# Down products of four feed-forward blocks: three groups of rows instead of two, placed in another order

## The chip, the cores and the metric

One core of one Trainium2 chip runs the kernel. The metric is the device time of one launch in microseconds (us); less is better. TensorE does the matrix products, VectorE (DVE) and ScalarE (ACT) the elementwise work, GpSimd (POOL) one small power function, and SyncE (SP) issues the transfers.

## What is computed

Two layers of an encoder on 512 positions of width 1024, in float32. Each layer is a feed-forward block, a mixing block and a second feed-forward block, each with an RMS norm ahead of it and a residual add behind it; a last RMS norm follows. The change concerns the four feed-forward blocks (width 2816):

```
def swiglu(h, w_gate, w_up, w_down):
    return (jax.nn.silu(h @ w_gate) * (h @ w_up)) @ w_down
...
    for l in range(DEPTH):
        x = x + 0.5 * swiglu(rmsnorm(x, g_ffn1[l]), w_ffn1_gate[l], w_ffn1_up[l], w_ffn1_down[l])
        ...                      # mixing block: Fourier, dilated and differential attention, gates
        x = x + 0.5 * swiglu(rmsnorm(x, g_ffn2[l]), w_ffn2_gate[l], w_ffn2_up[l], w_ffn2_down[l])
    return rmsnorm(x, g_final)
```

## The kernel before, in words

Activations lie with features on the 128 partitions and the 512 positions along the free axis. Each float32 operand is held as a high and a low part; a product is three matmuls (`mm3`, L186: low by high, high by low, high by high), all into one PSUM accumulator.

**Feed-forward block** (`ffn`, L533). The width 2816 is 22 blocks of 128, called rows here. For each row `tile_ops` (L541) pushes a gate product and an up product: 8 blocks of the input by 3 matmuls of 512 columns each, so 48 matmuls for a row. Behind the up product, `act` (L552) multiplies by the norm's row factors, applies silu and multiplies gate by up.

**Down products.** `FGROUPS` (L35) splits the 22 rows into (0, 12) and (12, 22). Behind the gate and up products of a group come its down products, in one of two forms.

- The form of seven products (`quad_ops`, L601): two output blocks and two rows at a time, with the positions in two halves of 256, done as 7 products in place of 8. `seven` (L340) builds sums and differences of two rows, with high and low parts, in 3.5 tiles of the `pairs` pool (21 buffers); `load` (L207) adds up the weights on DVE and splits 7 blocks into parts; the products go into 4 accumulators, and `combine` (L626) puts them together on DVE and adds to `x`. Output blocks come in 4 sets (o = 0, 2, 4, 6); a set is loaded in pieces of up to 4 rows.
- The plain form (`down_ops`, L575): one output block at a time, 3 matmuls per row. In the last block of the network it is done for each half of the positions by itself (256 columns), so that the final norm (`LastNorm`, L499) can begin on one half.

Before, all rows of the first three feed-forward blocks take the form of seven products; in the last block rows 0 to 11 do, and rows 12 to 21 are plain in halves.

**Order.** Work that needs weights is an `Op` in a queue (`push`, L258). `fill` (L277) takes one, emits the weight work of the next one too, then whatever waits in `later` (the `combine` of a finished set), then the products. Other work, such as the statistics of a norm, are generators (`spawn`, L263), each with a due time; `step` (L295) advances one when its due time is at or below `est.time`, the running sum of what matmuls are taken to cost. Due times come from `Estimate` and `_Engine` (L94 to L126), which add up costs of ACT and DVE instructions in the order in which they are emitted, each from the result of the one before (`est.ready`). `Norm.ready` (L475) drives a generator to its end at once, whatever its due time. At the end of a block `drain` (L306) empties the queue before the next block pushes its own.

**Norm.** When output block k of `x` is final, `Norm.block` (L471) makes its high and low parts (ACT, DVE) and adds its square to a sum (ACT, DVE). Behind the eighth block `square` (L450) spawns `stats` (L462): four small matmuls with ones, DVE, the power function on POOL, ACT, DVE (`diagonals`, L414), then two matmuls (`bcast`, L427) that spread the factors.

Of the kernel before, what the change touches and what calls it, by code (L numbers as in the profile page):

```python
# [14 lines left out]
ALU = mybir.AluOpType  # L15
# [19 lines left out]
FGROUPS = ((0, 12), (12, 22))  # L35
# [94 lines left out]
def encoder_kernel(ctx: ExitStack, tc: tile.TileContext, I: dict, out: bass.AP):  # L130
# [50 lines left out]

    def mm(ps, w, xx, start, stop, us):
        T.matmul(ps, w, xx, start=start, stop=stop)  # L183
        est.pe(us)

    def mm3(ps, w, xx, start, stop, us=0.216):  # L186

        mm(ps, w[1], xx[0], start, False, us)
        mm(ps, w[0], xx[1], False, False, us)
        mm(ps, w[0], xx[0], False, stop, us)  # L190

    class Op:
# [14 lines left out]
        def load(self, cuts=1):  # L207
# [3 lines left out]
            if self.sums:  # L211
# [6 lines left out]
                self.w = []  # L218
                for r in raws:
                    V.tensor_tensor(r[:, 4:6], r[:, 1:4:2], r[:, 0:1].to_broadcast([P, 2, P]), op=ALU.add)  # L220
                    V.tensor_tensor(r[:, 6], r[:, 4], r[:, 3], op=ALU.add)
                    V.tensor_tensor(r[:, 7], r[:, 6], r[:, 2], op=ALU.add)
                    w = [t.rearrange("p (s c) -> p s c", s=7) for t in self.parts(896)]
                    split(*w, r[:, 1:])
                    self.w.append(w)
# [8 lines left out]
            self.w = []  # L234
            for a in range(0, n, per):
                e = min(n, a + per)
                hi, lo = self.parts(e - a)
                self.w.append((hi, lo))
                some = max(1, cuts // 2)
                for c in range(some):  # L240
                    cs = slice((e - a) * c // some, (e - a) * (c + 1) // some)
                    split(hi[:, cs], lo[:, cs], raw[:, a:e][:, cs])
                    if cuts > 1:
                        yield
# [95 lines left out]
    def seven(te, to, share):  # L340
# [10 lines left out]
        A.activation(a[:, 0], te[:, 0], AF.Copy)  # L351
        V.tensor_tensor(s0[:, 0], te[:, 1], te[:, 0], op=ALU.subtract)
        V.tensor_tensor(s0[:, 1], te[:, 1], to[:, 1], op=ALU.subtract)
        A.activation(a[:, 1:3], to, AF.Copy)
        V.tensor_tensor(s1[:, 0], te[:, 0], s0[:, 1], op=ALU.subtract)
        V.tensor_tensor(s1[:, 1], to[:, 0], s1[:, 0], op=ALU.subtract)
        A.activation(sh[:, 0:2], s0, AF.Copy)
        V.tensor_tensor(a[:, 3], te[:, 0], f(a[:, 0]), op=ALU.subtract)
        A.activation(sh[:, 2:4], s1, AF.Copy)
# [74 lines left out]
    class Norm:  # L434
# [8 lines left out]
        def pairs(self, k):  # L443
            p = xpair()
            A.activation(p[:, 0], x[:, k, :], AF.Copy, scale=gain(self.i, k))
# [4 lines left out]
        def square(self, k):  # L450
            if self.n == 0:
                self.sum = npool.tile([P, 512], F32, tag="sum", name=nm("sum"))
                A.activation(self.sum, x[:, k, :], AF.Square)
            else:
                sq = tmp()
                A.activation(sq, x[:, k, :], AF.Square)
                V.tensor_add(self.sum, self.sum, sq)
            self.n += 1
            if self.n == KD:
                self.chain = spawn(self.stats(), est.ready)  # L460
# [72 lines left out]
    def ffn(l, which, norm, nxt):  # L533
# [3 lines left out]
        last = isinstance(nxt, LastNorm)  # L537
        forms = [not (last and j >= FGROUPS[1][0]) for j in range(NF)]
        share = []

        def tile_ops(j):  # L541
# [6 lines left out]
            def up(w):  # L548
# [3 lines left out]
                def act():  # L552
# [11 lines left out]
                    else:  # L564
                        hs[j] = b
                        e = j - j % 2
                        if hs[e] is not None and hs[e + 1] is not None:
# [7 lines left out]
        def down_ops(o, f0, f1, half=None):  # L575
            mid = (f0 + f1 + 1) // 2
            po = []
            cs = slice(0, 512) if half is None else slice(half * 256, half * 256 + 256)
            us = 0.216 if half is None else 0.108
# [18 lines left out]
            part(f0, mid)  # L598
            part(mid, f1)

        def quad_ops(o, f0, f1):  # L601
            po = []

            def part(a0, a1):
                def body(w):
# [3 lines left out]
                    if a1 == f1:  # L609
                        def done():  # L610
                            combine(po, o)
                            if f1 == NF:
                                nxt.block(o)
                                nxt.block(o + 1)

                        if f1 == NF and o == KD - 2:
                            done()
                        else:
                            later.append(done)
# [22 lines left out]

        for f0, f1 in FGROUPS:
            for j in range(f0, f1):
                tile_ops(j)
            if forms[f0]:
                for o in range(0, KD, 2):
                    quad_ops(o, f0, f1)
            else:
                for half in (0, 1):  # L650
                    for o in range(KD):
                        down_ops(o, f0, f1, half)
# [35 lines left out]
    def token_major(l, norm, name, n, evict):  # L688
# [3 lines left out]
        def body(kk):  # L692
            def go(w):
                if kk == 0:
                    ps.extend(acc() for _ in range(NTB))
                for tb in range(NTB):
                    for k2 in range(2):
# [3 lines left out]
                        mm3(ps[tb][:, :n], xx, ww, k == 0, k == KD - 1, 0.216 * n / 512)  # L701
# [575 lines left out]
```

## Time and profile before

| | |
|---|---|
| Median of 3 runs | 2508.38 us (2500.59, 2508.38, 2508.8) |
| Profiled execution, its own time | 2503.38 us |
| Span of its trace | 2501.5 us |
| Granted clock of TensorE, mean | 0.986 of full |
| TensorE matmul busy | 2440.1 us (98%), 12902 instructions |
| VectorE busy | 1653.8 us (66%) |
| ScalarE busy | 1079.3 us (43%) |
| Chain that ended last | 90% TensorE, 7% VectorE |

The busy time of an engine is the time in which it executed instructions; matmuls are pipelined, so their busy time overlaps and hides gaps shorter than one matmul. A granted clock below 1 in a stretch means that TensorE ran there at half of its full clock for a part of it: its two levels are 2.4 and 1.2 GHz.

### The profile page before, as it was taken

Reading aid. Unit: us, or ns where it says so; the run is one execution under the profiler, and the core shown is the slowest. Engines: PE = TensorE matmul, PEld = TensorE weight load, DVE = VectorE, ACT = ScalarE, POOL = GpSimd, SP = SyncE. Lnnn points to the kernel's source line nnn. Section 1 sums busy time; section 2 is a strip of 40 time slices with the busy share of each in tenths; the row PEclk is TensorE's granted clock in tenths of the full one; section 3 lists DMA queues with packets and bytes.
Section 4 is the critical chain, followed back from the end, with each engine's and each line's share of the span. In section 5 each row is a group of like instructions: output and inputs, shape, how many; then the busy total and the mean of one; then the engine's idle time right before and its main releaser. Section 6 shows DMA issues by size and latency. Waiting matters only on the chain.

```text
span 2501.5 us, 33775 instructions
## 1 busy us (share of the span) xinstructions
PE 2440.1 (98%) x12902; PEld 2099.5 (84%) x12902; DVE 1653.8 (66%) x3254; ACT 1079.3 (43%) x1858; POOL 20.6 (1%) x24
## 2 busy tenths in 40 slices
PE   8999999999999999999999999999999999999997
PEld 6788898878887888988978988888888878889887
DVE  5687694545776656866956867845467656568556
ACT  4343353544544434433533434445455444334344
POOL 0000000000000000000000000000000000000000
PEclk9999999999999999999999999999999999999998
DMA  4333233212321323332322332331222213324334
GB/s 147 130 108 122 81 108 111 80 61 83 103 76 59 97 93 101 84 120 81 108 91 89 97 118 84 107 115 60 74 94 87 90 44 113 99 80 118 101 94 142
DMA packets 88850, 240.85 MB, mean 96 GB/s; under 512 B 10009, under 2 KB 17945, under 8 KB 88688
## 3 DMA queue, kind: packets, MB, share of 16 engines
q1 hardware_dynamic: 88688, 238.69, 30.3%
q8 instruction: 101, 1.65, 0.3%
q14 instruction: 61, 0.50, 0.1%
HBM read 235.41 MB, written 6.91 MB: 97 GB/s over the span
## 4 chain that ended last, share of the span: by engine, by line
PE 90%; DVE 7%; ACT 1%; DMA 1%; issue 1%; POOL 0%; SPq 0%; POOLq 0%; ACTq 0%; DVEq 0%
PE acc L183 89%; DVE wlo L124 2%; DVE t L124 1%; DVE raw L124 1%; DVE pr L124 1%; PE acc L1006 1%; ACT pr L124 0%; DVE ta L124 0%; DVE x L124 0%; DVE sum L124 0%; DVE xs L124 0%; ACT ta L124 0%; PE acc L916 0%; DMA raw<-in_w_ffn_quad 0%; ACT whi L124 0%
## 5 line engine op out<-in xcount | busy, mean ns | idle before, releaser
L183 PE MATMUL acc<-xs,whi 128*128 128x512 f32 x4032 | 1246.4, 390 | 0.8 <-DVE xs L124 0.8
L124 ACT ACTIVATE whi<-raw 128x512 fp32r<-128x512 f32 (+4 forms) x902 | 588.7, 658 | 1019.1 <-PE acc L183 830.0
L124 DVE TENSOR_TENSOR wlo<-raw,whi 128x512 fp32r<-128x512 f32 (+4 forms) x902 | 648.5, 724 | 435.5 <-ACT whi L124 426.2
L183 PEld LDWEIGHTS acc<-xs,whi 128*128 128x128 f32 x4032 | 759.1, 188 | 160.4 <-DVE xs L124 2.4
L183 PE MATMUL acc<-xs,wlo 128*128 128x512 f32 x2016 | 790.5, 392 | 6.2 <-ACT xs L124 5.8
L183 PE MATMUL acc<-pr,whi 128*128 128x256 f32 (+1 forms) x3176 | 665.5, 308 | 0.0
L183 PEld LDWEIGHTS acc<-pr,whi 128*128 128x128 f32 x3176 | 521.9, 193 | 27.2
L183 PE MATMUL acc<-pr,wlo 128*128 128x256 f32 (+1 forms) x1588 | 491.3, 309 | 6.0 <-DVE wlo L124 6.0
L183 PEld LDWEIGHTS acc<-xs,wlo 128*128 128x128 f32 x2016 | 380.1, 189 | 89.5 <-ACT xs L124 7.0
L183 PEld LDWEIGHTS acc<-pr,wlo 128*128 128x128 f32 x1588 | 306.6, 193 | 22.5 <-DVE wlo L124 6.8
L124 DVE TENSOR_TENSOR t<-acc,rows 128x512 f32<-128x512 f32 x238 | 163.0, 688 | 174.9 <-PE acc L183 171.6
L183 PE MATMUL acc<-whi,xs 128*128 128x512 f32 (+1 forms) x512 | 156.0, 382 | 3.8 <-ACT whi L124 3.8
L124 DVE TENSOR_TENSOR raw<-raw 128x128 f32<-128x128 f32 (+1 forms) x468 | 141.4, 331 | 17.4 <-DMA raw<-in_w_ffn_quad 12.2
L124 ACT ACTIVATE pr<-t 128x512 fp32r<-128x512 f32 (+3 forms) x152 | 93.6, 616 | 109.8 <-DVE t L124 107.8
L183 PE MATMUL acc<-pr,pr 128*128 128x256 f32 (+2 forms) x624 | 114.8, 315 | 5.9 <-ACT pr L124 4.3
L183 PEld LDWEIGHTS acc<-whi,xs 128*128 128x128 f32 x512 | 97.3, 192 | 19.4 <-ACT whi L124 4.2
L183 PEld LDWEIGHTS acc<-pr,pr 128*128 128x128 f32 (+1 forms) x624 | 87.0, 196 | 20.1 <-issue 7.9
L183 PE MATMUL acc<-wlo,xs 128*128 128x512 f32 (+1 forms) x256 | 97.5, 381 | 0.0
L124 DVE TENSOR_TENSOR pr<-ta,pr 128x512 fp32r<-128x512 f32 (+1 forms) x124 | 84.0, 681 | 8.8 <-ACT pr L124 8.3
L124 DVE TENSOR_TENSOR pr<-t,pr 128x256 fp32r<-128x256 f32 (+2 forms) x124 | 76.4, 616 | 16.9 <-ACT pr L124 15.0
L124 ACT ACTIVATE pr<-ta 128x512 fp32r<-128x512 f32 (+1 forms) x124 | 76.6, 621 | 24.0 <-DVE ta L124 21.8
L124 DVE SCALAR_TENSOR_TENSOR t<-acc,t 128x256 f32<-128x256 f32 x168 | 74.0, 462 | 3.0 <-PE acc L183 1.1
(99 smaller groups left out, 1253.9 us busy)
## 6 DMA issues: line engine op xcount, KB each, us to landing
raw<-in_w_ffn_up SPq DMA_DIRECT2D x88, 512.0 KB, 3.2
raw<-in_w_ffn_gate SPq DMA_DIRECT2D x87, 512.0 KB, 3.3
raw<-in_w_ffn_quad SPq DMA_DIRECT2D x156, 256.0 KB, 2.7
raw<-in_w_gate SPq DMA_DIRECT2D x48, 512.0 KB, 3.2
raw<-in_w_in SPq DMA_DIRECT2D x28, 512.0 KB, 3.3
raw<-in_w_ffn_down SPq DMA_DIRECT2D x32, 320.0 KB, 3.0
raw<-in_w_a SPq DMA_DIRECT2D x16, 512.0 KB, 3.3
raw<-in_w_br_a SPq DMA_DIRECT2D x16, 512.0 KB, 3.3
```

What stands on the lines that cost most here:

```text
L124: return call(out, *args, **kwargs)
L183: T.matmul(ps, w, xx, start=start, stop=stop)
L1006: T.transpose(tr[:, c * P:(c + 1) * P], es[0][:, c * P:(c + 1) * P], ident)
```

## The change

Rows are grouped as 8, 8 and 6. The first two groups take the form of seven products in all four blocks; the last six rows are plain in all four (in halves of the positions in the last block, as before). The four sets of a group are no longer placed behind all of its gate and up products: each stands behind the gate and up products of one of the first four rows of the next group (rows 8 to 11 and rows 16 to 19). A plain down product is loaded in one piece of 6 rows, no longer in two of 5. For a set of seven the additions of both weight pieces now come ahead of both splits on DVE. The estimates change too: `beside` emits an ACT instruction without moving `est.ready`; `splits` takes weights as there from time 0; matmuls count as 0.228 us in place of 0.216; and a norm's statistics are due at most 6 us after `est.time`.

```
-FGROUPS = ((0, 12), (12, 22))
+FGROUPS = ((0, 8), (8, 16), (16, 22))
...
+    def beside(*args, **kwargs):
+
+        t = est.ready
+        A.activation(*args, **kwargs)
+        est.ready = t
+
+    def splits(parts, at):
+
+        ready = []
+        for (hi, lo, src), t in zip(parts, at):
+            est.ready = t
+            A.activation(hi, src, AF.Copy)
+            ready.append(est.ready)
+        for (hi, lo, src), t in zip(parts, ready):
+            est.ready = t
+            V.tensor_tensor(lo, src, f(hi), op=ALU.subtract)
...
-    def mm3(ps, w, xx, start, stop, us=0.216):
+    def mm3(ps, w, xx, start, stop, us=0.228):
...
-                self.w = []
+                at = []
                 for r in raws:
+                    est.ready = 0.0
                     V.tensor_tensor(r[:, 4:6], r[:, 1:4:2], r[:, 0:1].to_broadcast([P, 2, P]), op=ALU.add)
                     V.tensor_tensor(r[:, 6], r[:, 4], r[:, 3], op=ALU.add)
                     V.tensor_tensor(r[:, 7], r[:, 6], r[:, 2], op=ALU.add)
-                    w = [t.rearrange("p (s c) -> p s c", s=7) for t in self.parts(896)]
-                    split(*w, r[:, 1:])
-                    self.w.append(w)
+                    at.append(est.ready)
+                self.w = [[t.rearrange("p (s c) -> p s c", s=7) for t in self.parts(896)] for _ in raws]
+                splits([(*w, r[:, 1:]) for w, r in zip(self.w, raws)], at)
...
+            halves = [slice(a, min(n, a + per)) for a in range(0, n, per)]
+            self.w = [self.parts(h.stop - h.start) for h in halves]
+            if cuts == 1:
+                splits([(*w, raw[:, h]) for w, h in zip(self.w, halves)], [0.0] * len(halves))
...
-            A.activation(p[:, 0], x[:, k, :], AF.Copy, scale=gain(self.i, k))
+            beside(p[:, 0], x[:, k, :], AF.Copy, scale=gain(self.i, k))
...
-                A.activation(sq, x[:, k, :], AF.Square)
+                beside(sq, x[:, k, :], AF.Square)
...
-                self.chain = spawn(self.stats(), est.ready)
+                self.chain = spawn(self.stats(), min(est.ready, est.time + 6.0))
...
-        last = isinstance(nxt, LastNorm)
-        forms = [not (last and j >= FGROUPS[1][0]) for j in range(NF)]
+        forms = [j < FGROUPS[-1][0] for j in range(NF)]
...
                         e = j - j % 2
+                        if any(j in g[:1] for g in FGROUPS):
+                            share.clear()
                         if hs[e] is not None and hs[e + 1] is not None:
...
-            part(f0, mid)
-            part(mid, f1)
+            part(f0, f1)
...
-                        def done():
-                            combine(po, o)
-                            if f1 == NF:
-                                nxt.block(o)
-                                nxt.block(o + 1)
-
-                        if f1 == NF and o == KD - 2:
-                            done()
-                        else:
-                            later.append(done)
+                        later.append(lambda: combine(po, o))
...
+        downs = deque()
         for f0, f1 in FGROUPS:
             for j in range(f0, f1):
                 tile_ops(j)
+                if downs:
+                    quad_ops(*downs.popleft())
             if forms[f0]:
-                for o in range(0, KD, 2):
-                    quad_ops(o, f0, f1)
-            else:
-                for half in (0, 1):
-                    for o in range(KD):
-                        down_ops(o, f0, f1, half)
+                downs.extend((o, f0, f1) for o in range(0, KD, 2))
+        for half in (0, 1) if isinstance(nxt, LastNorm) else (None,):
+            for o in range(KD):
+                down_ops(o, f0, f1, half)
```

The ACT copies and squares in `seven` become `beside` in the same way.

## Rows read from the trace of the kernel before

**Rows 1.** The page: busy time of each engine, one line of transfers.

```profile
PE 2440.1 (98%) x12902; PEld 2099.5 (84%) x12902; DVE 1653.8 (66%) x3254; ACT 1079.3 (43%) x1858; POOL 20.6 (1%) x24
...
raw<-in_w_ffn_quad SPq DMA_DIRECT2D x156, 256.0 KB, 2.7
```

**Rows 2.** Timeline of TensorE: start, us, engine, line, operation, tiles, shape, count.

```profile
122.71 0.39 PE L183 MATMUL acc<-xs,wlo 128*128 128x512 f32 x1
...
124.07 0.39 PE L183 MATMUL acc<-xs,wlo 128*128 128x512 f32 x1
...
159.94 0.28 PE L183 MATMUL acc<-pr,wlo 128*128 128x256 f32 x1
...
161.02 0.28 PE L183 MATMUL acc<-pr,wlo 128*128 128x256 f32 x1
```

**Rows 3.** Busy time by stretch, around seven waits of TensorE: each engine, clock, DMA.

```profile
355.00:380.00 25.00, 20.99 (x155) 20.30 (x154) 22.59 (x46) 11.40 (x18) 0.00 (x0) 0.93 0.38 121
1230.00:1250.00 20.00, 17.71 (x145) 17.26 (x144) 19.65 (x41) 10.07 (x16) 0.00 (x0) 1.00 0.44 133
1590.00:1612.00 22.00, 18.50 (x137) 17.95 (x136) 20.09 (x41) 10.27 (x16) 0.00 (x0) 0.92 0.33 107
44.00:52.00 8.00, 5.76 (x18) 4.29 (x17) 5.48 (x10) 3.43 (x6) 0.97 (x1) 0.79 0.22 74
400.00:412.00 12.00, 8.68 (x40) 8.36 (x39) 7.30 (x14) 5.20 (x11) 1.26 (x1) 0.72 0.13 45
1280.00:1292.00 12.00, 8.65 (x36) 7.09 (x35) 5.98 (x12) 2.69 (x5) 1.38 (x1) 0.86 0.24 84
1634.00:1644.00 10.00, 6.69 (x32) 6.44 (x31) 7.18 (x13) 4.20 (x9) 1.19 (x1) 0.83 0.15 54
```

**Rows 4.** Timeline of TensorE at three of these waits; brackets: idle before, releaser.

```profile
359.24 0.39 PE L183 MATMUL acc<-pr,wlo 128*128 128x256 f32 x1 [1.71 <-DVE wlo L124]
...
374.40 0.96 PE L183 MATMUL acc<-whi,xs 128*128 128x512 f32 x3 [2.30 <-ACT whi L124]
...
400.34 0.95 PE L183 MATMUL acc<-ones,sum 128*128 128x1 f32 x8
404.60 1.19 PE L183 MATMUL acc<-pr,ones_r 128*128 128x512 f32 x2 [3.32 <-DVE pr L124]
```

**Rows 5.** Groups by line and shape, VectorE: busy us, mean ns, idle before.

```profile
L124 DVE TENSOR_TENSOR wlo<-raw,whi 128x896 fp32r<-128x896 f32 x156 | 167.8, 1085 | 19.5 <-ACT whi L124 19.2
L124 DVE TENSOR_TENSOR t<-acc,rows 128x512 f32<-128x512 f32 x238 | 163.0, 688 | 174.9 <-PE acc L183 171.6 <-ACT rows L124 2.8
...
L124 DVE TENSOR_TENSOR raw<-raw 128x128 f32<-128x128 f32 x312 | 83.6, 287 | 4.0
...
L124 DVE TENSOR_TENSOR raw<-raw 128x256 f32<-128x256 f32 x156 | 64.7, 420 | 13.4 <-DMA raw<-in_w_ffn_quad 12.2
...
L124 DVE SCALAR_TENSOR_TENSOR xs<-x,vecs,xs 128x512 fp32r<-128x512 f32 x48 | 35.7, 749 | 3.7 <-ACT xs L124 2.5
...
L124 DVE TENSOR_TENSOR wlo<-raw,whi 128x384 fp32r<-128x384 f32 x48 | 26.7, 558 | 40.0 <-ACT whi L124 39.2
```

**Rows 6.** Busy time by stretch in down products: sevens (two), plain in halves (third).

```profile
160.00:198.00 38.00, 38.00 (x311) 37.01 (x311) 34.14 (x77) 15.01 (x18) 0.00 (x0) 1.00 0.42 115
328.00:372.00 44.00, 42.29 (x352) 41.98 (x350) 43.84 (x94) 22.25 (x32) 0.00 (x0) 1.00 0.41 120
2430.00:2470.00 40.00, 40.00 (x336) 40.00 (x335) 27.18 (x62) 28.31 (x68) 0.00 (x0) 1.00 0.67 188
```

**Rows 7.** Timeline of VectorE behind the last down product: the final multiplications.

```profile
2490.94 2.07 DVE L124 TENSOR_TENSOR t<-x,acc 128x256 f32<-128x256 f32 x6
2493.22 4.83 DVE L124 TENSOR_TENSOR t<-x,acc 128x256 f32<-128x256 f32 x10 [0.21 <-DMA out<-t]
```

**Rows 8.** First norm: count, ns min/median/max, first and last start.

```profile
L183 PE MATMUL acc<-ones,sum x8: 164/250/250, 42.7 to 43.4; 128*128 128x1 f32 x8
L124 DVE TENSOR_TENSOR sum<-sum,t x7: 682/687/694, 12.7 to 21.2; 128x512 f32<-128x512 f32 x7
```

More of the change, by code (lines that the diff above doesn't have):

```diff
@@ L233, in load @@
             per = (self.nb + 1) // 2 * P
[L234 to L243, printed above, removed]
+            halves = [slice(a, min(n, a + per)) for a in range(0, n, per)]
+            self.w = [self.parts(h.stop - h.start) for h in halves]
+            if cuts == 1:
+                splits([(*w, raw[:, h]) for w, h in zip(self.w, halves)], [0.0] * len(halves))
+            else:
+                for (hi, lo), h in zip(self.w, halves):
+                    for c in range(cuts // 2):
+                        cs = slice(2 * per * c // cuts, 2 * per * (c + 1) // cuts)
+                        split(hi[:, cs], lo[:, cs], raw[:, h][:, cs])
                         yield
@@ L350, in seven @@
         te, to, s0, s1 = (t.rearrange("p (t c) -> p t c", t=2) for t in (te, to, tma(), tma()))
-        A.activation(a[:, 0], te[:, 0], AF.Copy)
+        beside(a[:, 0], te[:, 0], AF.Copy)
         V.tensor_tensor(s0[:, 0], te[:, 1], te[:, 0], op=ALU.subtract)
         V.tensor_tensor(s0[:, 1], te[:, 1], to[:, 1], op=ALU.subtract)
-        A.activation(a[:, 1:3], to, AF.Copy)
+        beside(a[:, 1:3], to, AF.Copy)
         V.tensor_tensor(s1[:, 0], te[:, 0], s0[:, 1], op=ALU.subtract)
         V.tensor_tensor(s1[:, 1], to[:, 0], s1[:, 0], op=ALU.subtract)
-        A.activation(sh[:, 0:2], s0, AF.Copy)
+        beside(sh[:, 0:2], s0, AF.Copy)
         V.tensor_tensor(a[:, 3], te[:, 0], f(a[:, 0]), op=ALU.subtract)
-        A.activation(sh[:, 2:4], s1, AF.Copy)
+        beside(sh[:, 2:4], s1, AF.Copy)
         V.tensor_tensor(b, to, f(a[:, 1:3]), op=ALU.subtract)
@@ L452, in square @@
                 self.sum = npool.tile([P, 512], F32, tag="sum", name=nm("sum"))
-                A.activation(self.sum, x[:, k, :], AF.Square)
+                beside(self.sum, x[:, k, :], AF.Square)
             else:
                 sq = tmp()
-                A.activation(sq, x[:, k, :], AF.Square)
+                beside(sq, x[:, k, :], AF.Square)
                 V.tensor_add(self.sum, self.sum, sq)
@@ L575, in down_ops @@
         def down_ops(o, f0, f1, half=None):
-            mid = (f0 + f1 + 1) // 2
             po = []
             cs = slice(0, 512) if half is None else slice(half * 256, half * 256 + 256)
-            us = 0.216 if half is None else 0.108
+            us = 0.228 if half is None else 0.12
             def part(a0, a1):
@@ L700, in go @@
                         ww = wk(w, k2, n)
-                        mm3(ps[tb][:, :n], xx, ww, k == 0, k == KD - 1, 0.216 * n / 512)
+                        mm3(ps[tb][:, :n], xx, ww, k == 0, k == KD - 1, 0.228 * n / 512)
                         yield
```

## The prediction

> **What bounds the kernel now.** I read the page first: TensorE is busy 98% of the span, VectorE 66% [rows 1]. That busy time is modelled for a pipelined engine, so I took its pace from the timeline. Where nothing holds it up, six matmuls of 512 columns start in 124.07 - 122.71 = 1.36 us, 0.2267 us each, and nine of 256 columns in 161.02 - 159.94 = 1.08 us, 0.120 us each [rows 2]. A gain can come from fewer columns, or from places where that pace breaks. Then I looked for those places, and tabulated busy time around them [rows 3]; idle is the width of a window less PE's busy time, and the clock column says what its halved clock lost (width times one less the clock).
>
> Three places are ends of feed-forward blocks (the first three rows of [rows 3]): 25.00 - 20.99 = 4.01 us, 2.29 us and 3.50 us idle, 9.8 us together, with 25 x 0.07 + 22 x 0.08 = 3.5 us of clock behind them: 13.3 us. The timeline says what is late there: low parts of weights from DVE in the last sets of seven, then the high part of the next block's first weights from ACT [rows 4].
>
> Four places are norms (the last four rows of [rows 3]). The small matmuls with ones run, and the matmuls that spread the result stand right behind them, with no other product between; TensorE idles 3.32 us while DVE builds the diagonal [rows 4]. The three between blocks idle 3.32 + 3.35 + 3.31 = 10.0 us and lose 12 x 0.28 + 12 x 0.14 + 10 x 0.17 = 6.7 us of clock: 16.7 us. The first norm of the kernel idles 2.24 us and loses 8 x 0.21 = 1.7 us: 3.9 us.
>
> **The change part by part.**
>
> *Columns.* Over all 8 output blocks, two rows cost 4 sets x 7 products x 3 = 84 matmuls of 256 columns as sevens (10.08 us), 8 x 2 x 3 = 48 of 512 plain (10.88 us), and 96 of 256 plain in halves (11.52 us). Three blocks move 3 row pairs from sevens to plain: 9 x 0.80 = +7.2 us. The last block moves 2 pairs from halves to sevens: 2 x 1.44 = -2.9 us. Sum: **+4.3 us**, TensorE's own work, which nothing hides.
> The Trainium skill (TensorE: Matmul & The Clock Gate, section "Wait — 56ns, not 53.3ns?") gives a warm matmul its columns at 2.4 GHz plus 2.5 ns, so 109 and 216 ns; by that estimate this term would be +8.1 us, so its rule speaks more against the change. The trace's 120 and 227 ns stand, since they are of these matmuls.
>
> *Ends of blocks.* DVE is the cause. The instructions of 512 columns take 0.69 us, of 256 columns 0.42 us [rows 5]. A weight piece of a set takes 0.42 + 2 x 0.287 + 1.085 = 2.08 us; `combine` 4 x 0.42 + 2 x 0.69 + 0.69 + 0.42 = 4.2 us. A set of the second group (10 rows) has 5 pieces, one `combine` and two norm blocks of 0.75 + 0.69 us: 17.5 us of DVE beside 105 x 0.120 = 12.6 us of TensorE. The windows agree: DVE is busy 43.84 of 44 us and TensorE idles [rows 6]. Behind the change the last work is plain: an output block takes 18 x 0.2267 = 4.08 us on TensorE and on DVE 2 x 0.558 + 0.69 + 0.75 + 0.69 = 3.25 us, and the norm's blocks come one at a time. Only the last block's residual add, parts and square are left behind the last product, beside the next block's first products, which read input block 0 first and block 7 some 5 us later. I take back 11 of the 13.3 us; the bounds are 0 (the next block's first weights still stand behind the norm's ACT work, and idle as long as now) and 13.3.
>
> *Norms.* The due time of the statistics came from an estimate in which ACT and DVE take turns; a set's 4 pieces or so ran it ahead of the real engines, so the small matmuls came late (at 400.34 us, 26 us after the next block's first product at 374.40 [rows 4]) and were then driven straight through. With the cap of 6 us and `beside` they go out within a few products of the block's end, and the matmuls that spread them several us later, with products between. I take back 14 of 16.7 us, bounds 0 and 16.7; and 2 of 3.9 at the first norm, where the cap also applies (0 to 3.9). What is added: small matmuls ahead of a sum that is not there make TensorE, which takes matmuls in order, wait for it. From the last product to the sum is one add, a part, a square and an add, some 3 us by [rows 5] with ACT taken like DVE; the cap is 6 us.
>
> *Sets between gate and up products.* Nothing is removed from TensorE, but DVE's load is spread. A row costs DVE 4 splits and 3 multiplications of 0.69 = 4.8 us, half of a `seven` (5 x 0.42 + 3 x 0.69 = 4.2) 2.1 us; a set of 8 rows 4 x 2.08 + 4.2 = 12.5 us. A row and a set together: 19.4 us of DVE in 48 x 0.2267 + 10.08 = 20.96 us of TensorE, 93%; with rows 16 to 19, which need one 0.69 us split in place of `seven`, 18.0 us or 86%. A set of 12 rows now needs 6 x 2.08 + 4.2 = 16.7 us beside 15.1 us of TensorE, 110%, and yet TensorE is busy all of 160 to 198 us with DVE at 90% [rows 6], because gate and up products before and after lend it room. With the additions of both weight pieces ahead of both splits, DVE adds while ACT makes the first high part; its waits there are 19.5 us in all 156 pieces [rows 5], off TensorE's path, so that edit alone gives nothing. So new waits should be small. Queued behind a waiting DVE instruction are the low parts of the next weights, and behind those TensorE: the price of one such wait in the trace is 1.71 us [rows 4]. The `pairs` pool fills to its 21 buffers at row 11 (14 of the first group, 7 new); the next `seven` then waits for the group's last set, but is first read four rows later, so that costs nothing. I take +3 us in all, bounds 0 and one 1.71 us wait for each of the 32 sets (55 us). Transfers: 256 KB pieces land in 2.7 us [rows 1] and are now issued between gate and up loads on SP, one Op ahead as before, with 5 us of products to cover them; 128 of them remain of 156. POOL's queue holds only the norm's power function; nothing is moved past it.
>
> *Last block, halves.* A plain output block in halves becomes 18 x 0.120 = 2.16 us of TensorE with 2 x 0.558 + 2 x 0.42 = 1.96 us of DVE (91%). Before, it was 3.6 us with 2 x (0.558 + 0.42) + 0.84 = 2.8 us (78%), with TensorE never idle and 188 GB/s of transfers [rows 6]; the bytes per us stay (6 rows in 2.16, 10 in 3.6). The last row's product is due 5 x 0.36 = 1.8 us into the first of them, and its silu, multiplication and split need about 3 us: +1.5 us once. The tail holds 16 final multiplications, of both halves, 7.1 us from 2490.94 to 2498.05 [rows 7]: the first half's are there only because its statistics were due late by the same estimate. With weights taken as there from time 0, they should go out during the second half: -3 us (0 to -3.5, and DVE's 9% of room is what they must fit).
>
> *Elsewhere.* The estimates steer the mixing blocks too; their order will shift. I take 0, with 5 us either way.
>
> **Sum.** +4.3 - 11 - 14 - 2 + 3 + 1.5 - 3 = -21.2 us, against the profiled execution's own 2503.4 us: 2482. The median of the runs shown is 5 us above that execution, so I forecast **2487 us** for the median.
>
> **The rivals.**
>
> *Norms stay late or stall earlier (0.20).* If the small matmuls go out before the sum exists, or are still driven straight through, the 16 us of norms stay and the rest comes: 2487 + 16 = 2503 us. For it: the due times are estimates and 6 us is close to the 3 us that the sum takes. Against: the first norm's last add starts at 21.2 us and its matmuls at 42.7 us [rows 8], so there are 20 us between too late and too early.
>
> *Ends of blocks stay (0.13).* The wait for the next first weights (2.30 us [rows 4]) is one of the queue, not of the sets: `drain` is still there. Then 11 us stay: 2498 us.
>
> *DVE becomes the bound between the sets (0.07), slower.* At 93%, with ACT's high part ahead of every low part, each of 32 sets could hold TensorE once, at 1.71 us [rows 4]: 55 - 3 more, so 2487 + 52 = 2539 us. It ends above the time before from about 0.75 us for each set ((2508 - 2484) / 32). Against it: 110% in the first group now, without a wait.
>
> *The whole forecast (0.60)*: 2472 to 2497: the elsewhere term's 5 us either way, and up to 10 us more where the partial terms come whole and the new waits stay out.
>
> **How the numbers follow.** A difference of 0.5%, 12.5 us, is about what a measurement of this kernel can tell from none; the lines are 2495.8 and 2520.9. Faster: nearly all of the forecast's case, a third of each of the first two rivals' spread: 0.58 + 0.11 = 0.69. Slower: 0.07. Same: 0.24. The range leaves out the slow rival and some of the low end: 2472 to 2504.
>
> **What would show it.** In the profile after: 32 x 84 + 288 = 2976 matmuls of 256 columns in down products in place of 39 x 84 + 480 = 3756; no idle at the three ends of blocks; products between the matmuls with ones and those that spread; DVE under 95% in the interleaved stretches, with TensorE at 0.120 and 0.2267 us pace; first half's final multiplications ahead of the last down product. It is wrong if TensorE waits for low parts of weights inside the interleaved rows, or for the sum of squares at norms.

## The result, and the profile after

The changed kernel takes 2438.27 us (median of 4 runs, 2437.88 to 2438.85) against 2504.49 us (4 runs, 2499.99 to 2508.8): a ratio of 0.9736, 95% interval [0.9713, 0.9759]. That is faster, as forecast, but 34 us below the forecast's range: by the profiled executions' own times it gained 2503.4 - 2438.1 = 65.3 us where the sum said 21.2.

The page of the kernel after: busy time by engine, the chain that ended last, transfers.

```profile
span 2436.1 us, 32920 instructions
PE 2417.4 (99%) x12554; PEld 2065.4 (85%) x12554; DVE 1626.7 (67%) x3172; ACT 1067.3 (44%) x1836; POOL 20.9 (1%) x24
...
PE 98%; DVE 1%; DMA 0%; issue 0%; SPq 0%; ACT 0%; POOLq 0%; DVEq 0%
...
raw<-in_w_ffn_quad SPq DMA_DIRECT2D x128, 256.0 KB, 2.7
raw<-in_w_ffn_down SPq DMA_DIRECT2D x40, 384.0 KB, 3.1
```

VectorE's share of the chain fell from 7% to 1%; the mean granted clock rose from 0.986 to 0.998. Where the waits of [rows 3] stood, the kernel after has (busy time by stretch: three ends of blocks with the norm behind each, the first norm, the first four rows that have a set beside them):

```profile
350.00:376.00 26.00, 26.00 (x119) 21.42 (x118) 18.37 (x30) 13.69 (x23) 0.74 (x1) 1.00 0.36 114
1210.00:1230.00 20.00, 20.00 (x93) 16.41 (x92) 12.74 (x21) 8.90 (x15) 1.39 (x1) 1.00 0.32 111
1555.00:1577.00 22.00, 22.00 (x102) 18.05 (x100) 16.41 (x27) 11.89 (x20) 0.00 (x0) 1.00 0.38 127
20.00:52.00 32.00, 32.00 (x146) 26.40 (x144) 20.50 (x37) 13.80 (x23) 1.01 (x1) 1.00 0.30 101
105.05:188.94 83.89, 83.89 (x529) 76.34 (x528) 68.31 (x136) 35.06 (x51) 0.00 (x0) 1.00 0.35 110
```

PE's first number equals the width in each, at full clock; DVE is at 68.31 / 83.89 = 81% in the rows with sets. At the norm that idled 3.32 us in [rows 4], TensorE's timeline of the kernel after:

```profile
373.32 0.61 PE L200 MATMUL acc<-whi,xs 128*128 128x512 f32 x2
373.93 1.05 PE L200 MATMUL acc<-ones,sum 128*128 128x1 f32 x8
374.84 0.48 PE L200 MATMUL acc<-whi,xs 128*128 128x512 f32 x1
...
385.81 0.39 PE L200 MATMUL acc<-wlo,xs 128*128 128x512 f32 x1
386.27 0.63 PE L200 MATMUL acc<-pr,ones_r 128*128 128x512 f32 x2
```

The matmuls with ones go out 3 us behind the block's start (26 us before), and products fill the 11 us until the factors are spread.

**Where the rest came from.** I cut the span at three marks in TensorE's timeline for each mixing block: its first product `whi,xs`; the first product `xs,w` behind its first run of output products (the Fourier and dilated work lies before this mark, the differential attention behind it); and the first gate product of the next block. The two mixing blocks of before, then those of after, as busy time by stretch:

```profile
374.40:600.30 225.90, 219.64 (x1103) 185.69 (x1104) 109.14 (x250) 94.28 (x177) 1.26 (x1) 0.95 0.26 83
600.30:895.20 294.90, 289.00 (x1345) 240.85 (x1345) 202.27 (x391) 144.28 (x272) 5.09 (x4) 0.98 0.27 86
1609.60:1828.70 219.10, 212.84 (x1104) 180.02 (x1105) 108.88 (x250) 94.46 (x177) 1.19 (x1) 0.99 0.26 86
1828.70:2123.70 295.00, 289.04 (x1345) 240.92 (x1344) 202.17 (x391) 144.17 (x272) 4.89 (x4) 0.98 0.26 86
```

```profile
370.80:578.60 207.80, 207.80 (x1083) 175.50 (x1082) 100.84 (x237) 91.96 (x172) 1.01 (x1) 1.00 0.26 86
578.60:864.10 285.50, 284.74 (x1346) 237.42 (x1346) 200.10 (x391) 143.84 (x272) 5.01 (x4) 1.00 0.27 88
1573.10:1780.90 207.80, 207.80 (x1083) 175.49 (x1082) 100.86 (x237) 91.99 (x172) 1.01 (x1) 1.00 0.26 86
1780.90:2066.30 285.40, 284.64 (x1345) 237.38 (x1344) 200.06 (x391) 143.79 (x272) 4.94 (x4) 1.00 0.26 88
```

The mixing blocks, in which the change edits no product, became 18.1 + 9.4 + 11.3 + 9.6 = 48.4 us shorter. The first halves of before hold 21 down products more, which ran behind the mark: 2 x 21 x 0.120 = 5.0 us that only moved. Two of the norms lie in them too: 6.6 us idle and 5.1 us of clock in [rows 3]. And of the 13.3 us at ends of blocks, 5.6 x 0.30 = 1.7 us of clock lie behind the first mark (374.40 to 380.00 us, where TensorE is never idle and the clock is 0.70). So 48.4 - 5.0 - 11.7 - 1.7 = **30 us** came from elsewhere in the mixing blocks: 11 in the first halves, 19 in the second. By the rows above, 5.9 + 10.3 = 16 us of it are idle time that went, and the rest is clock. (The clock's part in the first halves is loose: e5 below, the same program as before, took 4.6 us more for one of them.) The term for all of it in the sum was 0.

What changed there is the order. TensorE's groups by form from 445 to 505 us before, and from 400 to 500 us after (tiles, count, busy, mean ns, idle before):

```profile
L183 PE MATMUL acc<-xs,whi 128*128 128x512 f32 x96 | 29.5, 389 | 0.0
L183 PE MATMUL acc<-pr,pr 128*128 128x256 f32 x144 | 21.4, 296 | 2.9 <-ACT pr L124 2.2 <-DVE pr L124 0.7
L183 PE MATMUL acc<-xs,wlo 128*128 128x512 f32 x48 | 18.7, 389 | 0.0
```

```profile
L200 PE MATMUL acc<-xs,whi 128*128 128x512 f32 x96 | 29.6, 389 | 0.0
...
L200 PE MATMUL acc<-pr,pr 128*128 128x256 f32 x144 | 19.5, 285 | 0.0
L200 PE MATMUL acc<-xs,wlo 128*128 128x512 f32 x48 | 18.8, 392 | 0.0
```

The same 144 products with weights and 144 Fourier products. Before, the timeline shows the first kind without a break from 445.9 us, and then the second by itself:

```profile
478.06 0.61 PE L183 MATMUL acc<-xs,whi 128*128 128x512 f32 x2
478.51 3.15 PE L183 MATMUL acc<-pr,pr 128*128 128x256 f32 x25
481.87 0.86 PE L183 MATMUL acc<-pr,pr 128*128 128x256 f32 x5 [0.20 <-DVE pr L124]
482.57 0.28 PE L183 MATMUL acc<-zn,cosf 128*128 128x1 f32 x2
482.71 1.55 PE L183 MATMUL acc<-pr,pr 128*128 128x256 f32 x11
484.10 0.28 PE L183 MATMUL acc<-zn,cosf 128*128 128x1 f32 x2
484.23 2.51 PE L183 MATMUL acc<-pr,pr 128*128 128x256 f32 x19
487.57 1.82 PE L183 MATMUL acc<-pr,pr 128*128 128x256 f32 x10 [0.83 <-ACT pr L124]
```

A chain of small dependent steps has nothing beside it that could cover ACT and DVE. In the timeline of the kernel after, the two kinds are mixed:

```profile
473.21 0.62 PE L200 MATMUL acc<-xs,whi 128*128 128x512 f32 x2
473.66 0.88 PE L200 MATMUL acc<-pr,pr 128*128 128x256 f32 x6
474.38 0.28 PE L200 MATMUL acc<-zn,cosf 128*128 128x1 f32 x2
474.52 0.96 PE L200 MATMUL acc<-pr,pr 128*128 128x256 f32 x6
475.31 0.28 PE L200 MATMUL acc<-zn,cosf 128*128 128x1 f32 x2
475.45 0.48 PE L200 MATMUL acc<-xs,wlo 128*128 128x512 f32 x1
```

**The suspected cause** is in the kernel's own bookkeeping. `split` counts an ACT part, then a DVE part behind it, then the next ACT part behind that, as if the two engines took turns; nothing takes the estimate back, so `est.ready` drifts ahead of `est.time`. Added up as the program is generated, it stands 104 and 193 us ahead at the start of the two mixing blocks of before, and 2 us in the kernel after. Fourier groups are spawned with that time as due time; until it comes, `step` issues what is in the queue; when the queue is empty, `est.time` jumps to the due time and the chains run alone. Summed in the same way, these jumps come to 108 and 197 us in the first halves of the two mixing blocks of before and to 31.4 us in each second half; in the mixing blocks of after there is none.

### The profile page after: what moved, and what is told of

The parts are those of the page before. It is cut to its first block, busy times and chain, and to the rows that moved or that the text cites. A ratio compares the mean times of both kernels' runs of the same rounds, so it can differ in the third digit from the quotient of the medians.

```text
span 2436.1 us, 32920 instructions
## 1 busy us (share of the span) xinstructions
PE 2417.4 (99%) x12554; PEld 2065.4 (85%) x12554; DVE 1626.7 (67%) x3172; ACT 1067.3 (44%) x1836; POOL 20.9 (1%) x24
## 4 chain that ended last, share of the span: by engine, by line
PE 98%; DVE 1%; DMA 0%; issue 0%; SPq 0%; ACT 0%; POOLq 0%; DVEq 0%
PE acc L200 97%; DVE ta L124 1%; PE acc L1015 1%; PE acc L925 0%; DVE pr L124 0%; DMA x<-in_xT 0%; DVE t L124 0%; DVE wlo L124 0%; PE acc L928 0%; DMA out<-t 0%; DVE xs L124 0%; ACT xs L124 0%; SPq L1183 0%; DVE sum L124 0%; DVE z L124 0%
## 5 line engine op out<-in xcount | busy, mean ns | idle before, releaser
L124 ACT ACTIVATE whi<-raw 128x512 fp32r<-128x512 f32 (+4 forms) x890 | 578.4, 651 | 1013.9 <-PE acc L200 913.3
L124 DVE TENSOR_TENSOR wlo<-raw,whi 128x512 fp32r<-128x512 f32 (+4 forms) x890 | 633.6, 715 | 401.4 <-ACT whi L124 392.7
L200 PE MATMUL acc<-pr,whi 128*128 128x256 f32 (+1 forms) x2944 | 654.7, 318 | 0.0
L200 PEld LDWEIGHTS acc<-pr,whi 128*128 128x128 f32 x2944 | 489.2, 190 | 38.3
L200 PE MATMUL acc<-pr,wlo 128*128 128x256 f32 (+1 forms) x1472 | 469.9, 319 | 0.0
L200 PEld LDWEIGHTS acc<-pr,wlo 128*128 128x128 f32 x1472 | 280.4, 190 | 21.0 <-issue 0.7
L124 DVE TENSOR_TENSOR raw<-raw 128x128 f32<-128x128 f32 (+1 forms) x384 | 126.5, 333 | 28.8 <-DMA raw<-in_w_ffn_quad 23.0
L124 DVE SCALAR_TENSOR_TENSOR t<-acc,t 128x256 f32<-128x256 f32 (+1 forms) x192 | 85.3, 464 | 1.5
L124 DVE TENSOR_TENSOR pr<-ta,pr 128x512 fp32r<-128x512 f32 (+1 forms) x110 | 74.1, 683 | 5.9 <-ACT pr L124 5.2
L124 ACT ACTIVATE pr<-ta 128x512 fp32r<-128x512 f32 (+1 forms) x110 | 67.1, 619 | 19.6 <-DVE ta L124 19.4
```

Source lines behind the costliest of these rows:

```text
L124: return call(out, *args, **kwargs)
```

## The experiments

Each row is one kernel. The stages are those of the marks above, in us of the profiled execution; "last" is the last feed-forward block with the tail. Ratios are to the kernel before as run beside each one (its medians were 2501.5 to 2507.4 us), with the 95% interval.

| run | median us | ratio | to mixing 1 | its halves | between | mixing 2, halves | last |
|---|---|---|---|---|---|---|---|
| before | 2504.49 | 1 | 374.4 | 225.9, 294.9 | 714.4 | 219.1, 295.1 | 377.8 |
| after | 2438.27 | 0.9736 [0.9713, 0.9759] | 370.8 | 207.8, 285.4 | 709.0 | 207.8, 285.4 | 369.7 |
| e1 | 2449.60 | 0.9790 [0.9767, 0.9813] | 372.7 | 210.1, 285.5 | 709.7 | 210.1, 285.4 | 373.4 |
| e2 | 2492.23 | 0.9963 [0.9949, 0.9977] | 376.5 | 222.0, 295.0 | 713.7 | 216.4, 292.5 | 375.1 |
| e3 | 2497.98 | 0.9982 [0.9970, 0.9993] | 373.0 | 225.4, 290.8 | 715.1 | 226.3, 290.8 | 372.9 |
| e4 | 2452.00 | 0.9800 [0.9782, 0.9819] | 372.5 | 211.0, 286.7 | 709.4 | 211.0, 286.7 | 372.6 |
| e5 | 2501.35 | 1.0000 [0.9990, 1.0009] | 373.1 | 225.3, 294.8 | 714.1 | 223.7, 294.6 | 377.1 |
| e6 | 2477.36 | 0.9901 [0.9886, 0.9916] | 371.0 | 220.2, 286.6 | 714.0 | 223.4, 286.6 | 372.2 |
| e7 | 2501.55 | 0.9987 [0.9976, 0.9998] | 370.2 | 226.2, 294.9 | 714.2 | 223.8, 294.7 | 377.2 |
| e8 | 2480.24 | 0.9911 [0.9896, 0.9925] | 372.2 | 214.2, 292.4 | 708.4 | 215.7, 294.4 | 377.3 |
| e9 | 2511.91 | 1.0028 [1.0013, 1.0043] | 385.1 | 209.3, 300.6 | 731.4 | 208.3, 299.6 | 379.0 |
| e10 | 2440.28 | 0.9740 [0.9715, 0.9765] | 372.8 | 207.8, 285.4 | 710.4 | 207.8, 285.5 | 370.3 |
| e11 | 2440.62 | 0.9742 [0.9721, 0.9763] | 370.5 | 207.7, 286.6 | 709.0 | 207.7, 286.7 | 370.5 |
| e12 | 2439.75 | 0.9738 [0.9717, 0.9759] | 369.8 | 207.6, 285.5 | 707.1 | 207.6, 285.5 | 374.6 |
| e13 | 2477.22 | 0.9893 [0.9869, 0.9916] | 375.5 | 211.4, 294.6 | 708.8 | 210.0, 295.9 | 377.8 |
| e14 | 2437.89 | 0.9737 [0.9714, 0.9760] | 371.8 | 207.6, 285.4 | 708.6 | 207.6, 285.5 | 369.5 |
| e15 | 2463.94 | 0.9848 [0.9813, 0.9882] | 371.5 | 210.5, 290.6 | 708.6 | 211.9, 290.7 | 375.1 |
| e16 | 2460.20 | 0.9827 [0.9797, 0.9857] | 372.1 | 212.5, 286.6 | 709.5 | 215.2, 286.6 | 372.3 |
| e17 | 2435.17 | 0.9716 [0.9700, 0.9732] | 369.9 | 207.6, 285.4 | 707.1 | 207.6, 285.5 | 370.0 |

**Groups or estimates: e1 and e2.** e1 is the kernel before with every edit of the estimates and the old groups; e2 is the kernel after with every such edit taken back.

```
e1  -FGROUPS = ((0, 8), (8, 16), (16, 22))     (and ffn as before)
e2  -def beside(...) / splits(...) / min(est.ready, est.time + 6.0) / 0.228
```

> The kernel before with all four edits to the estimates (beside, splits with its order of the weight additions, 0.228 us, the cap of 6 us) and the old groups (0,12), (12,22) placed as before. Theory A (due times): the mixing blocks' 37 us beyond the norms, the norms' 20 us and the tail's 3 us come from the order that the estimates give, so about 2504 - 58 = 2446 us, and the waits for low parts of weights at the ends of feed-forward blocks stay. Theory B (groups): the sets' load on VectorE runs on into the mixing block, and it is the new groups that end it; then the estimates give the norms alone, about 2504 - 17 = 2487 us.

> The kernel after with all four edits to the estimates undone, so that groups, placement and plain last rows are all that is left. Theory A: 13 us of waits at the ends of blocks go, 4 us of columns come, so about 2495 us, with the waits in the mixing blocks as before. Theory B: about 2504 - 40 = 2464 us or less.

The estimates alone bring 2.1%, the groups alone 0.37%, of 2.6%. By the spans they gain 54.5 and 10.4 us, 64.9 of the 65.4 together, so they hardly act on each other. In e2 the waits at the ends of blocks are gone and nearly everything in the mixing blocks stays; in e1 it is the other way round (2.71 us of wait at 356.27 us, for one). The first end of a block in e2, as busy time by stretch:

```profile
350.00:380.00 30.00, 30.00 (x134) 24.83 (x133) 22.74 (x37) 16.93 (x30) 0.00 (x0) 1.00 0.38 114
```

e2's 9 us are the prediction's own terms: +4.3 for columns less 13.3 for the ends.

**One estimate at a time: e3, e4, e6, e7, e8.** On the kernel before: e3 only the cost of a matmul, e7 only `beside`, e6 only `splits`, e8 only the cap on the norm's due time; e4 the last three together.

```
e3  -us=0.216   +us=0.228
e6  -split(hi, lo, src)   +splits([...], [0.0] * n)
e7  -A.activation(...)   +beside(...)
e8  -spawn(self.stats(), est.ready)
    +spawn(self.stats(), min(est.ready, est.time + 6.0))
```

> The kernel before with one edit: a matmul of 512 columns counts as 0.228 us in the estimate in place of 0.216 (0.12 for 256). Theory A1: the running sum lags 5% behind TensorE, chains come late and the queue of products runs empty before them; the one figure gives the mixing blocks' 37 us, so about 2467 us. Theory A2: it is the estimated VectorE and ScalarE running ahead that makes chains late; then this alone gives under 10 us, 2495 us or more.

> The kernel before with beside, splits and the cap, but 0.216 us for a matmul. Theory A1: the norms alone, about 2504 - 17 = 2487 us. Theory A2: norms and mixing blocks, about 2450 us.

> The kernel before with splits alone (weight splits that do not wait for each other in the estimate, additions of both pieces ahead of both splits). The carried backlog falls from 104 and 193 us to 41 and 50 us. Theory A, where what counts is whether steps are due before the queue of products runs empty: most of the mixing blocks' 37 us, so 2470 us or less, with the norms after a feed-forward block still late (41 us is past the 22 to 33 us after which they are driven through). Theory A': a backlog over some 30 us is as bad as 190; about 2495 us.

> The kernel before with beside alone. Backlog 64 and 112 us. Theory A: some of the 37 us, between e6 and before, about 2485 us. Theory A': about 2498 us.

> The kernel before with the cap alone: a norm's statistics are due at most 6 us after the running sum. Only their first step moves; later steps still add to a backlog of 100 us and more, since each engine's next free time is in the estimate. Theory N1: the first step early is enough, the norms' 20 us go: about 2482 us. Theory N2: the steps behind it stay late through the backlog and are driven through, so under 6 us: 2496 us or more.

`splits` and the cap gain some 22 to 25 us each, by different ways. The cap clears the three norms between blocks. In the stretch of the first of them, busy time in e8:

```profile
374.00:410.00 36.00, 36.00 (x187) 32.19 (x186) 20.76 (x38) 13.95 (x26) 1.01 (x1) 1.00 0.33 114
```

Its first halves are 11.7 and 3.4 us shorter. That is idle at the norm and clock (1.00 and 0.99 there, 0.95 and 0.99 before), for the four waits at the Fourier groups are as they were (0.83, 0.70, 0.47 and 0.62 us, from 478.23 us on). Its second halves stay nearly as they were. `splits` clears most of the second halves (286.6) and leaves those norms. e3 and e7 gain next to nothing (0.9982 and 0.9987), so theory A2 of e3 held, and A' of e7 came nearer than A; yet e3, in which no split is edited, has second halves of 290.8 us. Busy time by stretch of e6, Fourier groups and differential attention (before: 22.06 of 25 at clock 0.98, and 34.10 of 40 at 0.87):

```profile
478.00:503.00 25.00, 22.52 (x158) 19.95 (x157) 18.39 (x69) 13.29 (x27) 0.00 (x0) 1.00 0.14 43
780.00:820.00 40.00, 38.49 (x186) 31.34 (x185) 20.99 (x37) 15.42 (x29) 1.01 (x1) 1.00 0.21 66
```

**Clearing the estimate itself: e5, e9, e13.** These edit no cost at all: e5 sets the engines' estimated free times back to `est.time` at the start of a mixing block; e9 and e13 do so at the eighth square of a norm, with the cap.

```
+for e in (V, A, G):
+    e.free = min(e.free, est.time)
e9   +est.ready = min(est.ready, est.time); spawn(self.stats(), min(est.ready, est.time + 6.0))
e13  +spawn(self.stats(), est.time + 6.0); est.ready = min(est.ready, est.time)
```

> The kernel before with one line: at the start of each mixing block the times at which the estimate holds ACT, DVE and POOL busy are set back to the running sum, if they are past it. In the kernel before they stand 104 us past it at the first mixing block and 193 us at the second. Theory A (carried backlog): it is this that makes every step of the mixing block late, so the 37 us of waits in the mixing blocks go and the norms at their start stay (their due time is set before): about 2502 - 37 = 2465 us. Theory C: the estimates go wrong inside the mixing block itself; then nothing much changes, over 2490 us.

> The kernel before with the backlog cleared where a block ends: behind the eighth square, the estimate's times for ACT, DVE and POOL and est.ready are set back to the running sum, and the cap is in. Nothing else of the change. At the Fourier groups the estimate is then 10 us ahead as in the kernel after, where e5 had 110 us, because there the norm's own late due time put the backlog back at once. Theory A, in two parts: the norms between blocks (17 us) and the Fourier groups (about 15 us: windows 480 to 515 and 1700 to 1740) are the carried backlog's and go; the waits at the differential attention's end (780 to 820, 2018 to 2048) come from the splits' turns inside the mixing block and stay: about 2502 - 32 = 2470 us. Theory A, one part: all 37 us and the norms go: about 2447 us. Theory D (the backlog is not it): 2480 us as with the cap alone.

> The kernel before with the cap on the norm's due time, and at a norm's eighth square the program's estimated free times of VectorE, ScalarE and GpSimd set back to the running sum, the norm itself due 6 us later. In the program's own sums the Fourier groups then begin 10 us late instead of some 110. Theory A (how late the estimates are when the Fourier groups are spawned decides the waits there, and clearing the lateness alone removes them): the Fourier half of a mixing block takes 208 to 211 us as in the kernel after (207.8), against 225.9 and 219.1 before; the differential half keeps its waits (292 to 295), since in it the estimates are late by the splits of its own weights; ends of FFN blocks keep theirs; about 2470 us. Rival B (the forced clearing at a norm makes PE wait for the norm's sum, whatever the due time, as the 6 us waits of the run before did): the sum of PE's waits of 3 to 6 us at each norm stays, and the time is 2490 or more.

e5 did nothing and tested nothing: the norm's due time, set earlier, still lay far ahead, and by the kernel's sums the Fourier groups were spawned 110 us late as before. Its program comes out as the same list of instructions as before, so its row shows how far repeats of one program lie apart: 223.7 us against 219.1 in the first half of the second mixing block. e9 was slower, against what I expected. Its first halves are short (209.3, 208.3), so the clearing worked there; but the norm's statistics were now due at once, and TensorE waited for the sum: one line of the timeline, and the busy time of the stretch around it.

```profile
383.36 1.87 PE L198 MATMUL acc<-ones,sum 128*128 128x1 f32 x8 [5.78 <-DVE sum L124]
```

```profile
380.00:392.00 12.00, 8.64 (x26) 7.20 (x27) 4.64 (x9) 2.51 (x5) 1.01 (x1) 0.57 0.12 34
```

That is the prediction's rival of the norm that stalls earlier. e13 leaves the norm due 6 us later and settles the first halves: 211.4 and 210.0 us, with no edit but the clearing and the cap, against 214.2 and 215.7 with the cap alone and 225.9 and 219.1 before. In e13's busy time by stretch the Fourier groups run without a wait (132 of their 144 products lie in the first window), and the differential attention waits as before:

```profile
405.00:480.00 75.00, 75.00 (x421) 67.46 (x419) 42.90 (x95) 36.77 (x66) 0.00 (x0) 1.00 0.30 99
780.00:820.00 40.00, 35.28 (x157) 29.57 (x158) 23.29 (x43) 14.90 (x28) 1.92 (x2) 0.87 0.12 39
```

The DMA share says it from the other side: 0.30 in the Fourier stretch here, 0.14 in e6's, where the queue had run out of products whose weights could load. The whole came out 7 us above the expected 2470: the wait at the first norm came back (3.36 us at 48.04 us) with the end of the first block.

**Taking one out of the kernel after, and adding up: e14, e15, e16, e11.** e14 is after without `beside`, e15 after without `splits`, e11 after with 0.216; e16 is before with cap and `splits`.

```
e14  -t = est.ready / est.ready = t     (in beside)
e15  -splits([...], at)   +split(hi, lo, src)
e11  -us=0.228   +us=0.216
```

> The kernel after with the copies and squares on ScalarE counted as before (a copy pushes the estimate of what follows on VectorE), all else as after. Theory A (only the lateness counts): the program's own sums are late by 6 us at the start of a mixing block, as little as in the kernel after, so 2436 to 2444 us and no wait in the mixing blocks. Rival C (each part of the change works in its own place, and this one is what brings the Fourier groups forward): the waits at the Fourier groups come back, 8 to 15 us in each of the two mixing blocks, 2455 to 2470 us.

> The kernel after with the splits of weights and sums counted as before (hi and lo parts one behind the other, from the estimate of whatever came last), all else as after. Theory A: the program's own sums are 31 and 43 us late at the start of the mixing blocks, it runs out of products ready to issue in the Fourier half and in the differential half, so part of the waits of both halves comes back; the differential half takes 290 to 295 us against 285.4, the Fourier half 212 to 218 against 207.8, 2455 to 2475 us. Rival C (the cap on the norm's due time is enough once the groups are of 8): no more than 2445.

> The kernel before with the cap and with the splits' estimates, old groups, copies counted as before. Theory A: the program's own sums are 41 and 47 us late at the start of the mixing blocks: the Fourier half keeps part of its waits (212 to 218 us), the differential half loses its (286), the norms lose theirs: 2460 to 2466 us, 8 to 14 more than with the copies' estimates as well (2452.0). Rival C (the two are enough, the copies' estimates are worth nothing): 2450 to 2455.

> The kernel after with 0.216 us for a matmul again. By e1 less e4 the figure is worth 2 us on top of the rest: about 2440 us. If the two are needed together with the groups, over 2445 us.

Theory A of these texts held three times (e15's first halves, 210.5 and 211.9 us, lie just under its 212 to 218). With the new groups `beside` is worth nothing (6 us of lateness at the mixing blocks, as harmless as 2); with the old ones it is worth 2455.0 - 2449.8 = 5.2 us by the spans of e16 and e4, whose sums are 41 and 47 us late, and 27. Their medians lie 8 us apart, but e16's four runs spread over 10, so the size is uncertain. Without `splits` the sums are 31 and 43 us late and 26 us come back, in both halves, at the Fourier groups and at the end of the last block. 0.228 is worth 2 to 4 us (e11, e1 against e4, e3), most of it in the second halves: 286.6 with `splits` alone, 285.4 with both.

**Placement and groups: e10, e12, e17.** e10 is after with the four sets of a group behind it, as before; e12 has groups of 8, 10 and 4; e17 has these in the first three blocks and 8, 8 and 6 in the last.

```
e10  -if downs: quad_ops(*downs.popleft())     +for o in range(0, KD, 2): quad_ops(o, f0, f1)
e12  -(8, 16), (16, 22)   +(8, 18), (18, 22)
e17  +groups = FGROUPS if isinstance(nxt, LastNorm) else ((0, 8), (8, 18), (18, 22))
```

> The kernel after with one edit: the four sets of a group of 8 stand behind the group's own gate and up products again, not between the next ones. A set takes VectorE 12.5 us beside 10.1 us of TensorE, 124%. Theory P1: TensorE waits for low parts of weights in most groups, 2 to 5 us in each of 8, so 2454 to 2478 us. Theory P2: the gate and up products before and after lend enough room, as for the first group of 12 rows in the kernel before; 2438 to 2442 us, and the placement is worth nothing by itself.

> The kernel after with groups of 8, 10 and 4 rows. Columns: one row pair more as sevens, 3 x 0.80 + 1.44 = 3.8 us less on TensorE. Theory Q1: TensorE's columns decide, 2434 us. Theory Q2: VectorE decides at the end of a block: a plain output block of 4 rows takes TensorE 2.72 us and VectorE 2 x 0.42 + 0.69 + 0.75 + 0.69 = 2.97 us, and in halves 1.44 us against 1.68 us, so 3 x 8 x 0.25 + 16 x 0.24 = 10 us of waits come: 2444 us.

> The kernel after with groups of 8, 10 and 4 rows in the first three feed-forward blocks and 8, 8 and 6 in the last one. The run with 8, 10 and 4 in all four gained 1.0 us up to the first mixing block and 1.9 us between the two, and lost 4.9 us behind the second, in the last block and its tail. If the columns are what gained (2 rows from the plain form to the form of sevens, 0.8 x 4 = 3.2 us less for a pair in 4 sets of 3 blocks at most 2.4 us) and the tail is what lost, this kernel keeps the gain without the loss: 2434.5 to 2436.5 us. If the last block lost through something carried in from the blocks ahead of it, it is 2438 or more.

Placing the sets between the next group's products, the most visible part of the change, is worth 2.0 us (2439.99 to 2441.86 against 2437.88 to 2438.85). In the first feed-forward block the timeline of e10 adds one wait, 1.34 us for DVE at 114.80 us. e12 gains 2.9 us ahead of the last block and loses 4.9 in it, but not by the waits at output blocks that its text expected: one of 0.70 us stands there, at 2398.74 us. Its loss is in the tail, where TensorE waits 3.42 us for the last sum, as in the kernel before (2423.36 us; before, 2487.01 us); e17 keeps the one without the other and is the fastest, 2435.17 us (2434.97 to 2435.9).

## Why the prediction was wrong in size

*Columns, +4.3: right.* The groups by form hold 1984 + 992 = 2976 matmuls of 256 columns in down products, as written, and the pace is unchanged. e17 moves one pair of rows back in three blocks: 3 x 0.80 = 2.4 us by the term, 2436.1 - 2433.2 = 2.9 by the spans.

*Ends of blocks, -11: right, and whole (-13.3).* The windows above have no idle, and e2 shows it with the groups alone. The rival that the queue keeps the wait fell.

*Norms, -14 and -2: right, and whole (-16.7 and -3.9).* e8 shows the cap as the cause at the three norms between blocks, without `beside`. At the first norm the cause was another than I wrote: the cap alone leaves the wait (2.24 us at 46.06 us in e8), `splits` alone ends it (e6). The rival of early stalls exists (e9), but 6 us clears it.

*New waits, +3: none.* In the rows with sets no wait of TensorE is over 0.3 us, so the rival with DVE as the bound fell too. DVE has 81% in the first four of them and not 93%, since my sum took each instruction at its whole duration, and in a row of them the next one begins earlier: six multiplications of 256 columns take 2.07 us [rows 7], 0.34 us each where I counted 0.42.

*Halves, +1.5: not seen*; from 2376 to 2423 us TensorE is busy all 47. *Tail, -3:* from the last down product to the end it is 2501.5 - 2482.6 = 18.9 us before and 2436.1 - 2423.8 = 12.3 after, so -6.6. The way was another than I wrote: all 16 final multiplications still stand behind the last product, but they begin 0.5 us behind it (2424.31 us) instead of 8.3 us (2490.94, [rows 7]), since the first half's statistics are no longer late.

***Elsewhere, "I take 0, with 5 us either way": this step failed.*** It gave -30 us, nearly half of the gain. The sum with the measured sizes is 4.3 - 13.3 - 16.7 - 3.9 - 6.6 - 30 = -66, against -65.4 between the spans. The runs show why the term was not 0: the drift that I had named as the cause of the late norms also set the due times of the Fourier groups and, within the mixing block, of the differential attention. e13 shows the first by clearing alone. For the second, one of the waits of before in TensorE's timeline:

```profile
810.52 1.22 PE L183 MATMUL acc<-pr,ones_r 128*128 128x512 f32 x2 [3.36 <-DVE pr L124]
```

The second halves follow the sum of the jumps of `est.time` within them, whichever edit sets it. No jump gives 285.4 to 285.5 us (after, e1, e10, e12, e14, e17), 8.9 us gives 286.6 to 286.7 (e4, e6, e11, e16), 21.1 us gives 290.6 to 290.8 (e3, e15), and 31.4 us gives 292.4 to 295.9 (before, e2, e5, e7, e8, e13; e9's 299.6 and 300.6 hold a wait of 2.92 us for a norm's sum besides). `splits` alone takes the jumps from 31.4 to 8.9, 0.228 alone to 21.1, and both together to none. Since 0.228 changes nothing but `est.time`, it is the due times that count there.

The trace of before had warned of it. By its page, span less busy time is 2501.5 - 2440.1 = 61.4 us, and the mean clock of 0.986 adds 2501.5 x 0.014 = 35.0: 96 us (after: 18.7 + 4.9 = 24). My list of waits held 13.3 + 16.7 + 3.9 = 34. I read the places that the change seemed to aim at and didn't ask where the other 62 us were; the stretches 478 to 503 us (22.06 of 25 busy) and 780 to 820 us (34.10 of 40 at clock 0.87) were there to be seen.

## What to carry to other kernels

Add up the bound engine's lost time over the whole span before listing waits, and account for the remainder: a change to a shared order or cost model acts on all of it. Where a program orders its work by its own estimates, check how far they run ahead of its clock at each stage; a part that is late in the books is issued when nothing is left to cover it, whatever the engines could do. The Trainium skill (Perfetto Trace Analysis, section "Optimization Strategy") advises to interleave stretches with different limits. The traces here agree where chains of small steps met products with weights (some 11 us in the first halves), and show 2 us where the stretches were already full (e10).

## What the hardware showed that was not expected

The same wait costs clock at one time and not at another. In e16 TensorE waits for DVE's low parts at the end of two feed-forward blocks, 2.73 us at 356.13 and 2.72 us at 1565.96. Behind each it waits once more, for ACT, 1.65 us at 372.12 and 1.96 us at 1580.78. Busy time by stretch around the four:

```profile
355.00:362.00 7.00, 5.87 (x36) 5.87 (x37) 5.91 (x12) 3.04 (x4) 0.00 (x0) 0.76 0.51 150
369.00:376.00 7.00, 5.35 (x40) 4.93 (x39) 5.67 (x12) 3.26 (x6) 0.00 (x0) 1.00 0.33 93
1565.00:1572.00 7.00, 6.04 (x50) 6.04 (x51) 6.90 (x14) 3.62 (x5) 0.00 (x0) 1.00 0.56 157
1579.00:1586.00 7.00, 5.22 (x26) 5.06 (x27) 4.74 (x9) 3.11 (x6) 0.00 (x0) 0.76 0.42 134
```

The mean granted clock is 0.76 at the first wait of one pair and at the second of the other, which means that TensorE ran at 1.2 GHz for a part of these windows, and 1.00 at the other two. Each pair lost 7 x 0.24 = 1.7 us, but at different waits. So one execution's clock behind one wait is a loose price for it.

The clock also goes with the spread of the runs. e15 took 2459.5 and 2460.6 us at a mean clock of 0.996, 2467.2 at 0.992 and 2470.5 at 0.991; e16 took 2455.6 and 2456.8 at 0.997, 2463.6 and 2466.0 at 0.993. 2460 x 0.005 = 12 us is about the whole spread of e15. The kernel after (0.998 to 0.999) lies within 1.0 us in 4 runs. What grants one run of a program less clock than the next, no run here shows.
